# Attention in a hybrid encoder layer: 32 steps with every engine's order written out

## The chip, the cores and the metric

One core of a Trainium2 chip runs the whole layer in one launch. The core has five engines that run side by side, each through its own instruction stream in order: TensorE (PE, matmuls and transposes), VectorE (DVE), ScalarE (ACT), GpSimd (POOL) and SyncE (SP, which here only starts DMAs). The metric is the device time of one execution in microseconds.

## The reference

The layer takes x, 1024 rows by 1024 columns in float32, and does three residual steps and a last norm:

```python
x = x + 0.5 * swiglu_half_step(x, ffn1_norm, ffn1_w_in, ffn1_w_out)
x = x + hybrid_mixer(x, ...)
x = x + 0.5 * swiglu_half_step(x, ffn2_norm, ffn2_w_in, ffn2_w_out)
x = rms_norm(x, final_norm)
```

The mixer projects the normed rows to a query (4 heads of 128), keys and values (2 heads each), and the inputs of a two-way gated recurrence (4 heads of 128). It then computes

```python
attn = rms_norm(softmax(q @ k.T) @ v, attn_out_gain)      # 1024 x 512
rec  = rms_norm(recurrence, rec_out_gain) * silu(g)       # 1024 x 512
return concatenate([attn, rec]) @ w_out                   # 1024 x 1024
```

The feed-forward width is 2816.

## The kernel before, in words

Every matrix product is made of three products of halves: each float32 operand is split into a rounded high part and the rest, and high×high, high×low and low×high are added in the same bank. A split is a cast on ACT and a subtraction on DVE. So twelve matmuls of 128 by 512 make one half of an output projection of 128 rows: 4 heads by 3 products.

The stages follow each other: first FFN, projection and recurrence, attention with both output projections, second FFN. Only the attention stage differs between the two kernels. It works on 32 steps `(tp, n, tt)`: four query tiles of 256 rows, four heads, two halves of 128 rows. One step is

- six score matmuls into `s` (two banks wide, tag "pp"), a row maximum on DVE (`nmax`), the exponential with its sum on ACT (`p`, `den`), the reciprocal on DVE (`rd`), and the scaling of `p`, one half on POOL and the other on ACT;
- eight transposes of `p` in two sets of four (`ptp`, tag "b"), each set split by ACT and DVE into `pT`;
- at the second step of a pair, 24 matmuls `pv` over the values, then gain and split (`oT`) and the squares (`sq`, summed in `ssq`).

Beside the steps lie the other parts of the output. For each of 8 tiles of 128 rows, the recurrence row `rg` (four loads, and one of its gate) is multiplied by the gate on POOL, transposed (`rT`), split (`recT`), projected (`py`, two halves of 12 matmuls) and added to the row `x` from `d["x1"]`; the row goes to `d["x2"]`. For each tile of attention output, `pa` is projected in two halves, scaled by `rs_ao` (from `oss`, the sum of squares) and added to the row from `d["x2"]`. Then `xn` is the normed row for the second FFN. Query tiles are loaded (`qraw`), transposed (`qTp`) and split (`qT`).

The order on each engine is not the order of the code alone: the layer on top of the language reorders the recorded instructions by its own priorities and estimates, so the order that counts is that of the built program. A block under `tc.high_priority()` is pulled forward, and `issue_after` (in the helper `behind`, line 96) keeps an instruction behind another. On-chip memory comes from pools with a number of buffers; a tile that reuses a buffer waits for the last reader of the one before. The output banks are two (tag "o"), the transposes' banks two ("b"), the score banks two ("pp").

In the code below, `softmax` (line 1172) yields between the two halves of the scores; the loop at line 1338 starts the scores two steps ahead (`stage_a(i + 2)`). The recurrence tile i is put out at step i (`rec_out`, line 1265) and both halves of an attention tile at u = 2 or 4 of the next query tile (`attn_out`). Functions that are called but not printed: `split` (cast on ACT, subtraction on DVE), `load_split` (a load and a split), `ps` (a bank of the named tag), and `rstd` (two small operations on DVE and POOL). Line numbers such as L1183 are lines of this kernel.

## Time and profile before

| what | us |
| --- | --- |
| median of 3 runs (1927.78 to 1929.05) | 1928.6 |
| profiled execution, its own time | 1929.75 |
| its span, from first to last instruction | 1927.6 |
| PE busy in the span | 1905.8 |
| attention, from the first scores of step 2 to the end of the last projection | 1054.2 to 1276.2 |

How to read it: busy time is the sum over instructions of an engine; idle time of PE in brackets is put down to what ended it ("<-DVE pT L1206" means that the subtraction of line 1206 was the last thing waited for). In a row of a timeline the first number is the start and the second the length from the first start to the modelled last end, so neighbouring rows on PE overlap a little. "SPq" is SP's queue of DMAs; "landing" counts from issue to the last byte.

### The profile page before, as it was taken

What the parts mean: (1) busy time and instruction counts of PE and PEld (TensorE: products, weight loads), DVE (VectorE), ACT (ScalarE), POOL (GpSimd) and SP (SyncE); (2) the same over time, 40 slices, a digit from 0 to 9 for tenths busy, and PEclk for the clock granted to TensorE, in tenths of its full rate; (3) what the DMA queues carried; (4) which work ended last, traced back from release to release, by engine and by line L of the source; (5) the groups of instructions that cost most, each with busy time, mean ns of one, the idle gap of its engine ahead of it and who ended that gap; (6) DMA issues with size and microseconds to landing.
All of it is one profiled execution on the core that took longest, in us unless ns stands there. A gap on an engine that the chain in (4) does not pass through costs nothing.

```text
span 1927.6 us, 26292 instructions
## 1 busy us (share of the span) xinstructions
PE 1905.8 (99%) x10025; PEld 1597.7 (83%) x10025; DVE 1250.9 (65%) x1578; ACT 802.1 (42%) x1280; POOL 714.1 (37%) x561
## 2 busy tenths in 40 slices
PE   9999999999999999999999999999999999999998
PEld 8888888887888788888888888888888888888886
DVE  8655676655985763677673566657556666558966
ACT  6333343334444432334344455644333333334434
POOL 2664545543670100010001324407554645426701
PEclk9999999999999999999999999999999999999999
DMA  8333333226874411122133452283423332258644
GB/s 263 107 122 106 99 121 101 69 104 245 274 246 133 151 45 44 45 83 83 44 95 111 153 174 77 99 273 99 142 88 109 99 115 82 88 199 297 218 120 164
DMA packets 212940, 254.78 MB, mean 132 GB/s; under 512 B 13495, under 2 KB 140748, under 8 KB 212814
## 3 DMA queue, kind: packets, MB, share of 16 engines
q1 hardware_dynamic: 203758, 222.69, 36.4%
q0 software_dynamic: 9056, 30.42, 4.0%
q8 instruction: 79, 1.29, 0.3%
q14 instruction: 47, 0.39, 0.1%
HBM read 182.79 MB, written 70.25 MB: 131 GB/s over the span
## 4 chain that ended last, share of the span: by engine, by line
PE 90%; DVE 4%; DMA 3%; issue 1%; ACT 1%; POOL 0%; SPq 0%; DVEq 0%; POOLq 0%; ACTq 0%
PE pa_ffn L298 17%; PE pd_ffn L298 11%; PE pya_ffn L684 7%; PE rec_ps L166 6%; PE pc_ffn L298 6%; PE pb_ffn L298 6%; PE pp_ffn L280 5%; PE pye_ffn L684 3%; PE pyd_ffn L684 3%; PE pyc_ffn L684 3%; PE aq_ps L831 2%; PE ri_ps L831 2%; PE pa L1243 2%; PE rgv_ps L831 2%; PE pv L1215 2%; PE s L1183 2%
## 5 line engine op out<-in xcount | busy, mean ns | idle before, releaser
L94 DVE TENSOR_TENSOR hl_in_ffn_A<-raw_in_ffn,hl_in_ffn_A 128x512 fp32r<-128x512 f32 x120 | 177.4, 1478 | 94.0 <-ACT hl_in_ffn_A L93 93.9
L298 PE MATMUL pa_ffn<-ffn_T,hl_in_ffn_S 128*128 128x512 f32 x960 | 236.8, 389 | 0.0
L298 PE MATMUL pd_ffn<-ffn_B,hl_in_ffn_S 128*128 128x512 f32 x936 | 225.7, 389 | 0.0
L298 PEld LDWEIGHTS pa_ffn<-ffn_T,hl_in_ffn_S 128*128 128x128 f32 x960 | 180.2, 188 | 37.4
L298 PEld LDWEIGHTS pd_ffn<-ffn_B,hl_in_ffn_S 128*128 128x128 f32 x936 | 175.7, 188 | 36.4
L93 ACT CAST hl_in_ffn_S<-s_ffn 128x512 fp32r<-128x512 f32 x160 | 99.0, 622 | 212.2 <-PE pd_ffn L298 159.0
L94 DVE TENSOR_TENSOR hl_in_ffn_S<-s_ffn,hl_in_ffn_S 128x512 fp32r<-128x512 f32 x160 | 140.9, 885 | 70.7 <-ACT hl_in_ffn_S L93 70.5
L94 DVE TENSOR_TENSOR hl_out_ffn_A<-raw_out_ffn_A,hl_out_ffn_A 128x1024 fp32r<-128x1024 f32 (+1 forms) x66 | 101.6, 1551 | 48.1 <-ACT hl_out_ffn_A L93 47.3
L93 ACT CAST hl_in_ffn_A<-raw_in_ffn 128x512 fp32r<-128x512 f32 x120 | 74.9, 625 | 137.1 <-PE pc_ffn L298 70.8
L94 DVE TENSOR_TENSOR hl_out_ffn_S<-raw_out_ffn_S,hl_out_ffn_S 128x512 fp32r<-128x512 f32 (+1 forms) x88 | 101.6, 1162 | 40.7 <-ACT hl_out_ffn_S L93 40.7
L166 PE MATMUL rec_ps<-hm,hl_rec_w 128*128 128x512 f32 x528 | 123.1, 392 | 0.8 <-DVE hm L145 0.4
L254 POOL TENSOR_TENSOR s_ffn<-s_ffn,raw_in_ffn 128x512 f32<-128x512 f32 x40 | 63.5, 1587 | 159.5 <-issue 104.6
L684 PE MATMUL pya_ffn<-hl_out_ffn_S 128*128 128x512 f32 x528 | 120.9, 390 | 0.1
L298 PE MATMUL pa_ffn<-ffn_B,hl_in_ffn_A 128*128 128x512 f32 x480 | 116.9, 389 | 0.0
L684 PEld LDWEIGHTS pya_ffn<-hl_out_ffn_S 128*128 128x128 f32 x528 | 99.0, 188 | 21.4 <-DVE hl_out_ffn_S L94 1.0
L166 PEld LDWEIGHTS rec_ps<-hm,hl_rec_w 128*128 128x128 f32 x528 | 98.4, 188 | 21.7 <-DVE hm L145 0.8
L298 PE MATMUL pc_ffn<-ffn_T,hl_in_ffn_A 128*128 128x512 f32 x480 | 115.9, 389 | 0.0
L298 PE MATMUL pb_ffn<-ffn_B,hl_in_ffn_A 128*128 128x512 f32 x480 | 115.3, 389 | 0.0
L93 ACT CAST hl_out_ffn_S<-raw_out_ffn_S 128x512 fp32r<-128x512 f32 (+1 forms) x88 | 73.4, 837 | 95.7 <-PE pya_ffn L684 38.6
L298 PEld LDWEIGHTS pc_ffn<-ffn_T,hl_in_ffn_A 128*128 128x128 f32 x480 | 90.1, 188 | 18.7
L298 PEld LDWEIGHTS pb_ffn<-ffn_B,hl_in_ffn_A 128*128 128x128 f32 x480 | 90.1, 188 | 18.7
L298 PEld LDWEIGHTS pa_ffn<-ffn_B,hl_in_ffn_A 128*128 128x128 f32 x480 | 90.0, 188 | 18.7
(288 smaller groups left out, 3809.4 us busy)
## 6 DMA issues: line engine op xcount, KB each, us to landing
raw_in_ffn<-in_ffn_w_in SPq DMA_DIRECT2D x88, 512.0 KB, 4.2
raw_out_ffn_S<-d_comb SPq DMA_DIRECT2D x88, 256.0 KB, 2.7
d_comb<-g_ffn POOLq DMA_DIRECT2D x80, 256.0 KB, 2.3
raw_out_ffn_A<-d_act SPq DMA_DIRECT2D x66, 256.0 KB, 5.1
ffn_kept<-in_ffn_w_out SPq DMA_DIRECT2D x65, 256.0 KB, 5.4
d_act<-g_ffn SPq DMA_DIRECT2D x60, 256.0 KB, 2.3
raw_out_ffn_A<-in_ffn_w_out SPq DMA_DIRECT2D x52, 256.0 KB, 5.4
x<-d_x SPq DMA_DIRECT2D x24, 512.0 KB, 4.2
```

The lines of the kernel that those rows point to most:

```text
L93: nc.scalar.copy(hl[:, 0, :], src)
L94: (lo_engine or nc.vector).tensor_sub(hl[:, 1, :], src, hl[:, 0, :].bitcast(F32))
L166: nc.tensor.matmul(out, hl[:, a, ks], h[half][b][:, k, cols], start=(k == 0 and i == 0), stop=(k == NK - 1 and i == 2),)
L254: nc.gpsimd.tensor_sub(s2, s1, a11)
L280: nc.tensor.matmul(halves(ps[j]), A[2 * j + k // 4][:, a, ks], B[k // 4][:, :, b, k % 4, lo:hi], start=(k == 0 and i == 0), stop=(k == NK ...
L298: nc.tensor.matmul(ps, A[:, a, ks], op(key)[:, b, k, :], start=(first and k == 0 and i == 0), stop=(k == 3 and i == 2), skip_group_check=True,
L684: nc.tensor.matmul(ps, hl[:, a, j * P : (j + 1) * P], hl[:, b, hi], start=(first and i == 0 and n == 0), stop=(i == last and n == 2), skip ...
L831: nc.tensor.matmul(ps[:, tt, :], h[half][a][:, k, ts], hl[j][:, b, ws], start=(k == 0 and i == 0), stop=(k == NK - 1 and i == 2),)
L1183: nc.tensor.matmul(ps[:, ks], qT[:, a, qs], kT[:, b, kv, ks], start=(i == 0), stop=(i == 2))
L1215: nc.tensor.matmul(ps, vt[:, j, a, vs], pT[j][:, b, i4, :], start=(st == 0 and i == 0), stop=(st == NT - 1 and i == 2),)
L1243: nc.tensor.matmul(py, lhs(a, n), units[n][:, b, ds], start=(n == 0 and i == 0), stop=(n == 3 and i == 2),)
```

## The change

The attention is written as 32 steps in a fixed order. A helper `run` chains each instruction behind the one recorded last on the same engine, so that the order of the code is the order on PE, ACT, DVE and POOL (DMAs are not chained). Within a step: three score matmuls of the step two ahead, four transposes, three more scores; then the small operations; then `oss`, and `pv` of the pair that ended one step earlier; then one of the output parts, either both halves of a recurrence tile (steps 0, 1, 3, 4, 5, 7, 9, 11) or one half of an attention tile (12 steps from 13 on); then the transposes of the next recurrence tile, and half of a query tile's transposes (at u = 2 and 4, in the output banks, where it was all eight in a score bank); then the other four transposes of the step.

The rows of the recurrence part get a second buffer (`x1=2`). The attention weights (`woa`) are requested at steps 2, 5, 8 and 10 and split at 4, 7, 12 and 13. At the end the projections of the last two tiles take heads 0 to 2 first and head 3 after the last `pv`. Instruction counts and sizes stay as they are on PE. In the diff, `free` does the same as `run` without the chain.

```diff
 LEVELS = (1, 2, 4, 8, 16, 32, 64)
+REC_STEPS = (0, 1, 3, 4, 5, 7, 9, 11)
+WOA_LOADS = (2, 5, 8, 10)
+WOA_EARLY = {13: 3}
+WOA_LATE = {4: 0, 7: 1, 12: 2}
+ATTN_HALVES = (13, 15, 16, 17, 19, 21, 23, 25, 27, 28, 29, 31)
...
+        last = {}
+
+        def run(engine, fn, *args, **kw):
+            with self.behind(last.get(engine)):
+                last[engine] = fn(*args, **kw)
+            return last[engine]
+
...
+        def q_turn(do, tp, raw, half, tag):
+            pt = self.ps(f"qTp{tp}_{half}", tag)[:, :512]
+            for m in range(2):
                 for tt in range(2):
-                    o, i = n * 256 + tt * P, tt * 512 + n * P
-                    nc.tensor.transpose(pt[:, o : o + P], raw[:, i : i + P], self.ident)
-            qT = pools["qT"].tile([P, 2, 1024], F32R, name=f"qT{tp}", tag="qT")
-            self.split(qT, pt)
-            return qT
-
-        def softmax(tp, n, tt, qT):
-
-            kv = n // (NQ // NKV)
-            nm = f"{tp}_{n}_{tt}"
...
+        def rec_turn(t):
+            rg = rows[t][0]
+            run("pool", nc.gpsimd.tensor_mul, rg[:, 0:512], rg[:, 0:512], rg[:, 512:])
             pt = self.ps(f"rT{t}", "o")
             for n in range(NREC):
                 ns = slice(n * P, (n + 1) * P)
-                nc.tensor.transpose(pt[:, ns], rg[:, ns], self.ident)
-            rT = pools["rT"].tile([P, 2, 512], F32R, name=f"recT{t}", tag="rT")
-            nc.scalar.mul(rT[:, 0, :], pt, self.rec_gain)
-            nc.vector.scalar_tensor_tensor(
-                out=rT[:, 1, :], in0=pt, scalar=self.rec_gain, in1=rT[:, 0, :].bitcast(F32),
-                op0=ALU.mult, op1=ALU.subtract,
-            )
-            project(
-                lambda a, n: rT[:, a, n * P : (n + 1) * P], units, f"py{t}",
-                lambda ds, py: nc.vector.tensor_add(x1[:, ds], py, x1[:, ds]),
-            )
-            nc.sync.dma_start(d["x2"][t], x1)
-
-        def attn_scale(tp, sq, tag="o"):
+                run("pe", nc.tensor.transpose, pt[:, ns], rg[:, ns], self.ident)
+            rT = recT[t] = pools["rT"].tile([P, 2, 512], F32R, name=f"recT{t}", tag="rT")
+
+            def evacuate():
+                run("act", nc.scalar.mul, rT[:, 0, :], pt, self.rec_gain)
+                run("dve", nc.vector.scalar_tensor_tensor, out=rT[:, 1, :], in0=pt, scalar=self.rec_gain,
+                    in1=rT[:, 0, :].bitcast(F32), op0=ALU.mult, op1=ALU.subtract)
+
+            return evacuate
+
+        def rec_half(t, dd):
+            py = self.ps(f"py{t}_{dd}", "o")
+            half_out(py, lambda x, n: recT[t][:, x, n * P : (n + 1) * P], rec_units, cols(dd))
+            x1 = rows[t][1][:, cols(dd)]
+
+            def evacuate():
+                run("dve", nc.vector.tensor_add, x1, py, x1)
+                if dd:
+                    nc.sync.dma_start(d["x2"][t], rows[t][1])
+
+            return evacuate
+
+        def out_scale(tp, do=run, tag="o"):
...
         for i, (tp, n, tt) in enumerate(seq):
-            if i + 4 < len(seq) and seq[i + 4][1:] == (0, 0):
-                qT[tp + 1] = q_tile(tp + 1)
-            if i + 2 < len(seq):
-                ahead = stage_a(i + 2)
-                next(ahead)
+            a, u = steps[i], i % 8
+            ahead = step(i + 2) if i + 2 < len(seq) else None
             if tt == 0:
-                both = self.hpool.tile([P, 2, 2, 4, 256], F32R, name=f"pT{tp}_{n}", tag="h")
-                pT[i] = [both[:, j] for j in range(2)]
-            pair = i - tt
-            transposed(p[i], pT[pair], tp, n, tt, 0)
-            if i + 2 < len(seq):
-                finish_a(i + 2, ahead)
-            transposed(p[i], pT[pair], tp, n, tt, 1)
-            if tt == 1:
-                values(tp, n, pT[pair], oT[tp], sq[tp])
-            if i < NT:
-                rec_out(i, rec_units, *(loaded if i == 0 else rec_loads(i)))
-            for where in {4: (whl,), 6: (whl,), NT + 1: (whl,), NT + 2: (gate,)}.get(i, ()):
-                self.gate, self.exp = self.step_load, self.last_exp
-                units.append(out_unit(0, len(units), "woa", *where))
-                self.gate = self.exp = None
-            u = i % 8
-            if tp > 0 and u in (2, 4):
-                half = (2, 4).index(u)
-                if half == 0:
-                    scale[tp - 1] = attn_scale(tp - 1, sq[tp - 1])
-                late.append(attn_out(tp - 1, half, oT[tp - 1], scale[tp - 1], units))
-            if tp > 0 and u in (4, 6):
-                half = (4, 6).index(u)
-                to_ffn(2 * tp - 2 + half, late.pop(0))
-
-        def last_scale():
-            if 3 not in scale:
-                with self.tc.high_priority():
-                    scale[3] = attn_scale(3, sq[3], "b")
-            return scale[3]
-
-        attn_out(3, 0, oT[3], last_scale, units, "pp")
-        attn_out(3, 1, oT[3], last_scale, units, "o", self.total)
+                pT = self.hpool.tile([P, 2, 2, 4, 256], F32R, name=f"pT{a.nm}", tag="h")
+            a.pT = pT
+            if u == 0 and tp < 3:
+                raw_q = q_load(tp + 1)
+            if i in WOA_LOADS:
+                j = WOA_LOADS.index(i)
+                raw_w[j] = request(0, j, "woa")
+            if ahead:
+                scores(run, ahead, 0)
+            turned(a, 0)()
+            if i == 0:
+                rec_turn(0)()
+            if i in WOA_EARLY:
+                j = WOA_EARLY[i]
+                units.append(cast(raw_w.pop(j), j, *(gate if j == 3 else whl)))
+            if ahead:
+                scores(run, ahead, 1)
+            if i and i + 1 < len(seq):
+                scaled(run, steps[i + 1])
+            if ahead:
+                exponential(run, ahead)
+            after = []
+            if tp and u == 2:
+                after.append(out_scale(tp - 1))
+            if tt == 0 and waiting:
+                after.append(values(waiting))
+                waiting = None
+            outs = []
+            if i in REC_STEPS:
+                t = REC_STEPS.index(i)
+                if t + 1 < NT:
+                    rows[t + 1] = rec_loads(t + 1)
+                outs = [rec_half(t, dd) for dd in range(2)]
+            elif i in ATTN_HALVES:
+                t, dd = divmod(ATTN_HALVES.index(i), 2)
+                outs = [attn_half(t, dd)]
+            later = []
+            if i + 1 in REC_STEPS:
+                later.append(rec_turn(REC_STEPS.index(i + 1)))
+            if tp < 3 and u in (2, 4):
+                later.append(q_turn(run, tp + 1, raw_q, u // 2 - 1, "o"))
+            tb = turned(a, 1)
+            for f in outs:
+                f()
+            if ahead:
+                inverse(run, ahead)
+            for f in (*after, tb, *later, *finishing):
+                f()
+            finishing = []
+            if i + 1 in ATTN_HALVES[::2]:
+                row(ATTN_HALVES.index(i + 1) // 2)
+            if i - 1 in ATTN_HALVES[1::2]:
+                finishing.append(to_ffn(ATTN_HALVES.index(i - 1) // 2))
+            if i in WOA_LATE:
+                j = WOA_LATE[i]
+                units.append(cast(raw_w.pop(j), j, *(gate if j == 3 else whl)))
+            if tt:
+                waiting = a
+
+        t0 = 2 * (len(seq) // 8 - 1)
+        wide = {}
+        row(t0)
+        for t in (t0, t0 + 1):
+            wide[t] = self.ps(f"pa{t}")
+            for dd in range(2):
+                half_out(wide[t][:, cols(dd)], lhs_attn(t), units, cols(dd), range(3))
+            if t == t0:
+                values(waiting)()
+                finish = to_ffn(ATTN_HALVES.index(len(seq) - 1) // 2)
+        finish()
+        row(t0 + 1)
+        for dd in range(2):
+            half_out(wide[t0][:, cols(dd)], lhs_attn(t0), units, cols(dd), (3,))
+        out_scale(t0 // 2, run, "b")()
+        for dd in range(2):
+            attn_add(t0, dd, wide[t0][:, cols(dd)])
+        nc.gpsimd.dma_start(d["x3"][t0], rows[NT + t0])
+        for dd in range(2):
+            half_out(wide[t0 + 1][:, cols(dd)], lhs_attn(t0 + 1), units, cols(dd), (3,))
+        for dd in range(2):
+            attn_add(t0 + 1, dd, wide[t0 + 1][:, cols(dd)])
+        nc.gpsimd.dma_start(d["x3"][t0 + 1], rows[NT + t0 + 1])
...
-                c3, tc, "m2", rg=2, x1=1, rT=1, p=3, qT=2, qr=1
+                c3, tc, "m2", rg=2, x1=2, rT=1, p=3, qT=2, qr=1```

The built order shows what moved. The first place is PE at the start of the loop, from the scores of step 2 on (`s_1_0` is head 1, half 0; `ptp_0_0_0` the first four transposes of step 0; `py_0` the first half of recurrence tile 0). Before:

```order
L1183 MATMUL s_1_0_8672<-kT,qT_8611 128x512 x6
L1183 MATMUL s_1_1_8741<-kT,qT_8611 128x512 x6
L1202 MATMUL ptp_0_0_0_8677<-ident,p_0_0_8633 128x128 x4
L1202 MATMUL ptp_0_0_1_8696<-ident,p_0_0_8633 128x128 x4
L1183 MATMUL s_2_0_8845<-kT,qT_8611 128x512 x6
L1202 MATMUL ptp_0_1_0_8745<-ident,p_0_1_8649 128x128 x4
L1202 MATMUL ptp_0_1_1_8764<-ident,p_0_1_8649 128x128 x4
L1183 MATMUL s_2_1_8922<-kT,qT_8611 128x512 x6
L1271 MATMUL rT_8704<-ident,rg_8614 128x128 x4
```

Now, the same place:

```order
L1146 MATMUL s_1_0_8677<-kT,qT_8602 128x512 x3
L1146 MATMUL ptp_0_0_0_8681<-ident,p_0_0_8635 128x128 x4
L1146 MATMUL rT_8689<-ident,rg_8617 128x128 x4
L1146 MATMUL s_1_0_8677<-kT,qT_8602 128x512 x3
L1146 MATMUL py_0_8713<-hl_wor_8566,recT_8694 128x512 x3
```

The transposes of the first recurrence tile stand behind three scores and four transposes; before, they stood behind 24 scores and 16 transposes.

The second place is PE in step 4 of the changed kernel, between two sets of transposes (`py_0` and `py_1` are the halves of recurrence tile 3, whose four heads follow each other; `rT_9064` belongs to tile 4, `qTp_1` to the second half of the next query tile):

```order
L1146 MATMUL pv_1_1_9004<-pT_1_0_8828,v_attn 128x256 x24
L1146 MATMUL py_0_9037<-hl_wor_8566,recT_8967 128x512 x3
L1146 MATMUL py_0_9037<-hl_wor_8571,recT_8967 128x512 x3
L1146 MATMUL py_0_9037<-hl_wor_8576,recT_8967 128x512 x3
L1146 MATMUL py_0_9037<-hl_wor_8581,recT_8967 128x512 x3
L1146 MATMUL py_1_9050<-hl_wor_8566,recT_8967 128x512 x3
L1146 MATMUL py_1_9050<-hl_wor_8571,recT_8967 128x512 x3
L1146 MATMUL py_1_9050<-hl_wor_8576,recT_8967 128x512 x3
L1146 MATMUL py_1_9050<-hl_wor_8581,recT_8967 128x512 x3
L1146 MATMUL rT_9064<-ident,rg_9029 128x128 x4
L1146 MATMUL qTp_1_9070<-ident,qraw_8674 128x128 x4
```

All of these use the two output banks, and each waits for the last reader of what stood in its bank before; in the built program `py_1` waits for the add of `py_0`, and `rT_9064` for the add of `py_1`.

The third place is SP's queue at the end of the stage (`x_6` and `x_7` are the last two rows, `xn_` and `raw_in` loads of the second FFN). Before:

```order
L1296 DMA x_5_10602<-d_x_82 128x1024
L1545 DMA xn_3_10888<-d_xn_84 128x1024
L1296 DMA x_6_10768<-d_x_82 128x1024
L1296 DMA x_7_10804<-d_x_82 128x1024
L1545 DMA xn_0_10879<-d_xn_84 128x1024
```

Now:

```order
L1340 DMA x_5_10613<-d_x_82 128x1024
L1664 DMA xn_0_10890<-d_xn_84 128x1024
L1664 DMA xn_1_10891<-d_xn_84 128x1024
L241 DMA raw_in_ffn_0_0_10894<-in_ffn_w_in 128x8x128
L241 DMA raw_in_ffn_0_1_10896<-in_ffn_w_in 128x8x128
L1664 DMA xn_2_10898<-d_xn_84 128x1024
L1664 DMA xn_3_10899<-d_xn_84 128x1024
L241 DMA raw_in_ffn_1_0_10902<-in_ffn_w_in 128x8x128
L241 DMA raw_in_ffn_1_1_10904<-in_ffn_w_in 128x8x128
L1340 DMA x_6_10742<-d_x_82 128x1024
L241 DMA raw_in_ffn_2_0_11453<-in_ffn_w_in 128x8x128
L1340 DMA x_7_10820<-d_x_82 128x1024
```

The two rows moved behind eight and nine loads of the next stage.

More of the change, by code (lines that the diff above doesn't have):

```diff
@@ L1254, in rec_loads, with half_out @@
+            return evacuate
+        def half_out(py, lhs, units, ds, heads=range(4)):
+            for n in heads:
+                for i, (x, y) in enumerate(((0, 0), (0, 1), (1, 0))):
+                    run("pe", nc.tensor.matmul, py, lhs(x, n), units[n][:, y, ds],
+                        start=(n == 0 and i == 0), stop=(n == 3 and i == 2))
+        cols = lambda dd: slice(dd * 512, (dd + 1) * 512)
         def rec_loads(t):
```

257 lines of the change are left out of this document (143 added, 114 removed).

## The prediction

> **What bounds the kernel now.** I read the page first, for the engine that sets the end:
>
> ```profile
> span 1927.6 us, 26292 instructions
> PE 1905.8 (99%) x10025; PEld 1597.7 (83%) x10025; DVE 1250.9 (65%) x1578; ACT 802.1 (42%) x1280; POOL 714.1 (37%) x561
> PE 90%; DVE 4%; DMA 3%; issue 1%; ACT 1%; POOL 0%; SPq 0%; DVEq 0%; POOLq 0%; ACTq 0%
> ```
>
> TensorE is busy for 99% of the span and carries 90% of the chain of waits. The change touches the attention alone, so next come the windows over it (length, then PE, PEld, DVE, ACT and POOL busy, granted clock, DMA share, GB/s):
>
> ```profile
> 1054.20:1151.00 96.80, 94.19 (x539) 80.79 (x538) 58.60 (x87) 51.97 (x88) 32.67 (x24) 1.00 0.51 172
> 1151.00:1235.00 84.00, 81.47 (x513) 71.89 (x512) 55.16 (x86) 51.34 (x96) 34.82 (x34) 1.00 0.24 82
> 1235.00:1276.20 41.20, 39.75 (x232) 33.65 (x231) 22.67 (x40) 18.86 (x36) 10.50 (x12) 1.00 0.54 169
> ```
>
> Of 222.0 us PE is busy 94.19 + 81.47 + 39.75 = 215.4: **6.6 us of idle in the whole attention**. The waits of PE from there to the first matmuls of the second FFN (total, times, longest) name most of it:
>
> ```profile
> PE ptp L1202 <- DVE pT L1206: 3.2, 5, 1.0
> PE s L1183 <- ACT p L1190: 1.0, 2, 0.7
> PE rT L1271 <- issue: 0.9, 1, 0.9
> PE pv L1215 <- DVE pT L1206: 0.7, 2, 0.3
> PE pp_ffn L280 <- DVE ffn_B L388: 0.5, 1, 0.5
> ```
>
> With the last row, 7.1 us can be won. DVE, ACT and POOL have slack, but only if PE meets their results late. The clock is 1.00 throughout.
>
> **What the change costs.** The instructions of PE are the same in number and size, so its work stays and the time moves by the change of its idle: minus 7.1, plus what the new order waits for. Every engine now runs in the recorded order, so a late result stops all that stands behind it.
>
> *Step 0.* PE's row is three scores, four transposes, then the four rT transposes.
>
> ```profile
> 1054.29 2.89 PE L1183 MATMUL s<-kT,qT 128*128 128x512 f32 x12
> 1058.71 1.66 PE L1183 MATMUL s<-kT,qT 128*128 128x512 f32 x6 [0.66 <-ACT p L1190]
> 1062.46 0.60 PE L1271 MATMUL rT<-ident,rg 128*128 128x128 f32 x4
> 1055.11 0.36 SPq L1086 DMA_DIRECT2D d_g<-rg  x1
> 1057.47 0.43 SPq L1260 DMA_DIRECT2D rg<-d_g  x1
> rg<-d_g SPq DMA_DIRECT2D x1, 256.0 KB, 2.8
> 1060.63 1.29 POOL L1267 TENSOR_TENSOR rg<-rg 128x512 f32<-128x512 f32 x1
> ```
>
> Twelve scores take 1057.01 − 1054.29 = 2.72 us (2.89 less the tail that overlaps the next row), 0.227 each. PE is at the rT transposes at 1054.29 + 3 × 0.227 + 0.5 = 1055.5. Their input cannot be there: SP still writes the last gate at 1055.11, issues the gate load at 1057.47, it lands 2.8 later, and the product takes POOL 1.29: 1061.6. PE idles **6.2 us** (6.0 if the load lands sooner, 6.9 if POOL starts at 1060.63 and the 0.9 of issue returns). Before, 12 more scores, 12 more transposes and a wait of 0.66 lay there. Behind rT stand the other scores, the exponential of them and the projection, so nothing can fill it.
>
> *Steps 0 to 13.* The prices of what PE now meets directly (the last row is an add at the end of the stage; its matmuls ended at 1276.18, so a hand-over between engines takes 0.2):
>
> ```profile
> L1273 ACT ACTIVATE recT<-rT,cols 128x512 fp32r<-128x512 f32 x8 | 5.7, 706 | 2.0 <-PE rT L1271 2.0
> L1274 DVE SCALAR_TENSOR_TENSOR recT<-rT,cols,recT 128x512 fp32r<-128x512 f32 x8 | 6.0, 745 | 1.3 <-ACT recT L1273 1.3
> L1280 DVE TENSOR_TENSOR x<-py,x 128x512 f32<-128x512 f32 x16 | 11.0, 690 | 21.8 <-PE py L1243 11.7 <-DMA x<-d_x 5.4 <-PE ptp L1202 4.8
> L1221 ACT ACTIVATE oT<-pv,cols 128x256 fp32r<-128x256 f32 x16 | 7.6, 474 | 25.8 <-PE pv L1215 25.8
> L1230 ACT ACTIVATE sq<-pv 128x256 f32<-128x256 f32 x12 | 4.8, 396 | 1.9 <-DVE oT L1222 1.8
> L93 ACT CAST hl_woa<-raw_woa 128x1024 fp32r<-128x1024 f32 x4 | 4.2, 1053 | 6.4 <-DMA raw_woa<-in_w_out_mix 6.4
> L94 DVE TENSOR_TENSOR hl_woa<-raw_woa,hl_woa 128x1024 fp32r<-128x1024 f32 x4 | 4.9, 1221 | 3.1 <-ACT hl_woa L93 3.1
> 1276.38 0.75 DVE L1299 SCALAR_TENSOR_TENSOR x<-pa,rs_ao,x 128x512 f32<-128x512 f32 x1 [0.62 <-PE pa L1243]
> ```
>
> In step 0 three scores (0.7) cover recT's 0.706 + 0.745: wait 0.75. In step 4 the second py half takes the bank of the first, just ended: its add of 0.69 and two hand-overs of 0.2 stop PE for 1.05 or so, and the next rT waits as long for the second: 2.1. The query transposes of steps 2 and 10 stand in pv's bank, one set of four transposes behind pv: 0.474 + 0.396 + hand-overs − 0.4, 0.95 and 1.15. Step 13's projection needs the weight splits of steps 12 and 13, two casts and two subtractions in a chain with the softmax of the step: 2.2. Smaller ones, recT behind the step's casts on ACT and DVE: 0.6, 0.55, 0.55, 1.8 and 0.55 in steps 3, 5, 7, 9 and 11. The sum is **11.2**. One late engine catches up while PE waits for another, so I take 8.5; the ends are 3 (only steps 4 and 0) and 13.
>
> *Steps 14 to 31.* The bank for the next query transposes in step 18 is that of oss, and rs_ao stands on DVE behind these:
>
> ```profile
> L1205 ACT CAST pT<-ptp 128x512 fp32r<-128x512 f32 x64 | 36.8, 590 | 38.2 <-PE ptp L1202 38.2
> L1206 DVE TENSOR_TENSOR pT<-ptp,pT 128x512 fp32r<-128x512 f32 x64 | 43.2, 685 | 11.6 <-ACT pT L1205 11.2
> L1187 DVE TENSOR_REDUCE nmax<-s 128x1 f32<-128x1024 f32 x30 | 36.5, 1218 | 3.9 <-PE s L1183 3.6
> L1190 ACT ACTIVATE p<-s,nmax 128x1024 f32<-128x1024 f32 x30 | 33.9, 1131 | 0.8 <-DVE nmax L1187 0.8
> L125 DVE SCALAR_TENSOR_TENSOR xn_n<-x,rs_n,g_ffn_norm 128x1024 f32<-128x1024 f32 x6 | 7.7, 1283 | 3.5 <-POOL rs_n L86 3.5
> ```
>
> From the last transposes of step 17: 0.59 + 0.685 + 1.283 (xn) + 0.685 + 1.218 + 1.131 and some 1.0 of read, reciprocal and hand-overs = 6.6; PE has 6 scores, 4 transposes and pv, 4.7: wait 1.9. In the pairs after it, pv's 13th matmul needs the subtraction of the step before, which stands behind a reciprocal, and so behind the exponential; where xn (1.283) lies ahead too, the slack is gone: 0.25 to 1.3 at seven places, 5.5 in all. Sum **7.4**; I take 4.5, ends 1 and 9.
>
> *The tail.*
>
> ```profile
> 1248.41 11.83 SPq L1296 DMA_DIRECT2D x<-d_x  x2
> x<-d_x SPq DMA_DIRECT2D x2, 512.0 KB, 4.1
> 1260.99 1.16 PE L1202 MATMUL ptp<-ident,p 128*128 128x128 f32 x8 [0.18 <-DVE pT L1206]
> 1263.02 3.02 PE L1215 MATMUL pv<-pT,v_attn 128*128 128x256 f32 x23 [0.34 <-DVE pT L1206]
> 1270.59 5.75 PE L1243 MATMUL pa<-hl_woa,oT 128*128 128x512 f32 x24
> 1276.18 1.91 PE L442 MATMUL pt_ffn_B<-ident,xn 128*128 128x128 f32 x16
> 1278.83 1.94 PE L280 MATMUL pp_ffn<-ffn_B,hl_in_ffn_A 128*128 128x256 f32 x14 [0.45 <-DVE ffn_B L388]
> ```
>
> Before, the last two rows of x were requested ahead of the next stage's loads (both by 1259.92, the end of that issue row less 0.3). Now they stand in SP's queue behind xn_0 to xn_3 and four weight loads, x_7 even behind a fifth, which waits for a split on DVE. On DVE the four adds (0.75 each) stand ahead of the ffn_B splits that the first pp needs. Counted from the last ptp (which ends near 1262.0): heads 0 to 2 of pa6 and pv take PE 18 × 0.227 + 2.9 = 7.0; the oT step and two splits behind it (0.5 + 1.4) free SP at about 9; x_7 lands 4.1 later at best, at 13, and at 17 if its load takes twice as long beside four weight loads of its size. The adds cannot start before the sums of oss either, behind x_7's heads 0 to 2 and x_6's last head (24 × 0.227 = 5.4) and 1 of scale: 13.5. Four adds then end at 16.5, or at 18.5 with the late landing; two ffn_B splits and a hand-over bring the first pp to 18 to 20.5, and to 23 if both the splits and xn_5, which stand between on DVE, come late too. PE's own work to there is 24 pv, 48 pa and 16 transposes, 2.9 + 10.9 + 1.9 = 15.7: a wait of 2 to 8. I take **4.5**, nearer the low end, since x_7's landing is the one link that no row prices under this load.
>
> Sum: 6.2 + 8.5 + 4.5 + 4.5 − 7.1 = **+16.6 us**. On the profiled execution's own time of 1929.75 that is 1946.4; the median lies 1.15 below it, so **1945**. With all low ends: 12.2 − 7.1 = +5.1, 1934; with all high ends 36.9 − 7.1 = +29.8, 1958.
>
> **Rivals.**
> *A: not slower.* Scores two steps ahead hide every evacuation, the adds and casts come in time, and only step 0's 6.2 + 0.75 is left against the 7.1 won: 6.95 − 7.1 = −0.15, 1928.4. Faster than that only if the gate load lands sooner too: 1924 with 4 of the 6.2 gone. For it: DVE busy for only 58.60 of 96.80 us. Against: the bank of step 4 is a wait with no work between. Chance 0.17.
> *B: step 0 and the tail alone.* 6.2 + 0.75 + 4.5 − 7.1 = +4.4: 1933. For it: in most steps 2 us of scores and transposes lie between a result and its user. Chance 0.2.
> *C: the forecast*, 0.45.
> *D: the gaps slow PE's restart.* The first transposes of the program and later ones:
>
> ```profile
> 5.83 2.82 PE L1473 MATMUL warm<-ident 128*128 128x128 f32 x12
> 31.96 1.91 PE L442 MATMUL pt_ffn_B<-ident,x_late 128*128 128x128 f32 x16
> ```
>
> At the start one takes 0.235, later 0.12. If each of the two gaps, step 0's and the tail's, cost one to two times what those 12 lost (12 × 0.116 = 1.4), the forecast rises by 3 to 6, to about 1950. No gap inside the attention before is longer than 1.0, so its trace cannot decide. Chance 0.08.
> The Trainium skill (TensorE: Matmul & The Clock Gate, Part 1) says that the clock falls to half after an idle window of about 3.4 us and returns after as long a busy one; the two start rows agree in ratio. By it step 0 alone would cost an estimated 1.7 us more.
> *E: lag adds up.* ACT or DVE falls behind over a pair and no step gives it back: the high ends, 1958. Chance 0.1.
>
> **How the numbers follow.** C is the likeliest, so 1945. Its own range is 1938 to 1952; with B and D inside and the far halves of A and E left out, **1930 to 1957**. About 0.2% (3.9 us) is what can be told from no change. Faster: the part of A in which the early product or the gaps come back, 0.1. Same: the rest of A and a sliver of B, 0.09. Slower: 0.81.
>
> **What would show it.** In the new profile: a gap of about 6 us on PE at the first rT, ended by POOL; PE idle in the attention of 20 us or more against 6.6; py and rT waiting for adds in step 4; the first pp waiting for DVE behind an add of x_7 that a DMA released. I am wrong if the first rT's gap is under 3 us, or if PE's idle there is under 10.

## The result, and the profile after

The changed kernel takes **1954.07 us** (median of 4 runs, 1953.00 to 1954.73) against 1928.52 (4 runs, 1927.78 to 1929.05): a ratio of 1.0132, 95% interval 1.0115 to 1.0150, so 25.5 us slower. The forecast was 1945, 16.5 us slower, with 1930 to 1957 as its range. The direction and the kind of the losses came as forecast; the size did not, and the tail is where most of the difference lies.

The page of the changed kernel, the lines that answer to those of before:

```profile
span 1951.8 us, 26283 instructions
PE 1911.3 (98%) x10025; PEld 1598.6 (82%) x10025; DVE 1251.3 (64%) x1582; ACT 802.0 (41%) x1284; POOL 714.9 (37%) x561
PE 86%; DVE 6%; DMA 3%; ACT 3%; issue 1%; POOL 0%; SPq 0%; DVEq 0%; POOLq 0%; ACTq 0%
```

The span grew by 24.2 us with the same 10025 matmuls; PE's share of the chain fell from 90% to 86%. Where PE waited from the start of the attention to the first matmuls of the second FFN (total, times, longest):

```profile
PE pt_ffn_B L447 <- DVE x L1146: 7.9, 2, 4.5
PE rT L1146 <- POOL rg L1146: 6.0, 1, 6.0
PE qTp L1146 <- DVE rs_ao L1146: 2.0, 1, 2.0
PE qTp L1146 <- ACT ssq L1146: 1.9, 2, 1.1
PE pa L1146 <- DVE hl_woa L1146: 1.2, 2, 0.8
PE py L1146 <- DVE recT L1146: 1.0, 3, 0.3
PE py L1146 <- ACT recT L1146: 1.0, 1, 1.0
PE rT L1146 <- issue: 0.8, 1, 0.8
PE py L1146 <- DVE x L1146: 0.8, 1, 0.8
PE pv L1146 <- DVE pT L1146: 0.6, 2, 0.3
```

Two rows hold 13.9 of some 23 us: the gap of step 0 and the transposes of the second FFN (`pt_ffn_B`), which wait for the adds on the last two rows of x. (L1146 is the line through which every operation of the fixed order is issued; tiles tell them apart.)

**Step 0** on PE, and the granted clock there (windows: length, PE, PEld, DVE, ACT, POOL busy, clock, DMA share, GB/s):

```profile
1061.85 1.12 PE L1146 MATMUL rT<-ident,rg 128*128 128x128 f32 x4 [6.03 <-POOL rg L1146]
1064.05 7.42 PE L1146 MATMUL py<-hl_wor,recT 128*128 128x512 f32 x24
1071.31 0.60 PE L1146 MATMUL rT<-ident,rg 128*128 128x128 f32 x4
```

```profile
1062.00:1066.00 4.00, 4.00 (x12) 3.24 (x13) 1.88 (x2) 2.33 (x3) 1.29 (x1) 0.50 0.35 96
1066.00:1068.00 2.00, 2.00 (x6) 1.56 (x6) 0.00 (x0) 0.86 (x2) 0.00 (x0) 0.56 0.46 125
1068.00:1072.00 4.00, 4.00 (x23) 3.31 (x22) 1.18 (x2) 0.00 (x0) 0.00 (x0) 1.00 0.01 4
```

The gap is 6.03 us long, ended by POOL's product, as forecast. Behind it the clock stands at half for some 5 us, and the 24 matmuls of the first projection take 7.42 us.

**The tail.** SP's queue, then DVE's adds, then PE:

```profile
1259.44 16.61 SPq L1664 DMA_DIRECT2D xn<-d_xn  x2
1276.10 1.28 SPq L241 DMA_DIRECT2D raw_in_ffn<-in_ffn_w_in  x2
1284.68 3.48 SPq L1340 DMA_DIRECT2D x<-d_x  x1
1288.77 1.58 SPq L1340 DMA_DIRECT2D x<-d_x  x1
```

```profile
1293.39 1.41 DVE L1146 SCALAR_TENSOR_TENSOR x<-pa,rs_ao,x 128x512 f32<-128x512 f32 x2 [4.38 <-DMA x<-d_x]
1298.73 1.41 DVE L1146 SCALAR_TENSOR_TENSOR x<-pa,rs_ao,x 128x512 f32<-128x512 f32 x2 [3.93 <-DMA x<-d_x]
```

```profile
1274.99 0.60 PE L1146 MATMUL ptp<-ident,p 128*128 128x128 f32 x4
1300.19 1.12 PE L447 MATMUL pt_ffn_B<-ident,xn 128*128 128x128 f32 x4 [3.37 <-DVE x L1146]
1300.96 3.20 PE L285 MATMUL pp_ffn<-ffn_B,hl_in_ffn_A 128*128 128x256 f32 x15
```

The first pp before:

```profile
1278.00 0.38 PE L280 MATMUL pp_ffn<-ffn_B,hl_in_ffn_A 128*128 128x256 f32 x1
```

And the chain that ended last, over the same stretch:

```profile
1276.57 9.21 DMA raw_in_ffn<-in_ffn_w_in
...
1288.77 9.84 DMA x<-d_x
```

SP stands at the second xn load for 16 us, and what ended most of that is named in the view of SP's waits:

```profile
SPq L1664 <- PE ptp L1146: 15.8, 1, 15.8
```

It waits for the last transposes of p, since the place it loads into still holds the last step's probabilities. Only then do the weights start; they land 9.21 later; the split and xn follow on DVE, then the request of x_7, which lands 9.84 later; and the transposes of the next stage need the banks that x_7's adds still read. From the end of the last score transposes (1274.99 + 0.60) to the first `pp_ffn` it is 25.4 us, for the 15.7 us of PE's own work that the prediction counts there (24 pv, 48 pa, 16 transposes). Before it was 1278.00 − 1262.15 = 15.9, but with 39 of the 48 pa: the other 9 stood ahead of the last score transposes. (The first pp row before is one matmul ahead of the row that the prediction shows.)

### The profile page after: what moved, and what is told of

Read it like the earlier page. It is cut to its first block, busy times and chain, and to the rows that moved or that the text cites. A ratio compares the mean times of both kernels' runs of the same rounds, so it can differ in the third digit from the quotient of the medians.

```text
span 1951.8 us, 26283 instructions
## 1 busy us (share of the span) xinstructions
PE 1911.3 (98%) x10025; PEld 1598.6 (82%) x10025; DVE 1251.3 (64%) x1582; ACT 802.0 (41%) x1284; POOL 714.9 (37%) x561
## 3 DMA queue, kind: packets, MB, share of 16 engines
q8 instruction: 79, 1.29, 0.3%
## 4 chain that ended last, share of the span: by engine, by line
PE 86%; DVE 6%; DMA 3%; ACT 3%; issue 1%; POOL 0%; SPq 0%; DVEq 0%; POOLq 0%; ACTq 0%
PE pa_ffn L303 17%; PE pd_ffn L303 11%; PE pya_ffn L689 7%; PE rec_ps L171 6%; PE pc_ffn L303 6%; PE pb_ffn L303 6%; PE pp_ffn L285 5%; PE pye_ffn L689 3%; PE pyc_ffn L689 3%; PE pyd_ffn L689 3%; PE py L1146 2%; PE aq_ps L836 2%; PE ri_ps L836 2%; PE rgv_ps L836 2%; PE pyb_ffn L689 2%
## 5 line engine op out<-in xcount | busy, mean ns | idle before, releaser
L99 DVE TENSOR_TENSOR hl_out_ffn_S<-raw_out_ffn_S,hl_out_ffn_S 128x512 fp32r<-128x512 f32 (+1 forms) x88 | 108.0, 1239 | 37.8 <-ACT hl_out_ffn_S L98 37.8
L99 DVE TENSOR_TENSOR hl_out_ffn_A<-raw_out_ffn_A,hl_out_ffn_A 128x1024 fp32r<-128x1024 f32 (+1 forms) x66 | 95.7, 1463 | 52.6 <-ACT hl_out_ffn_A L98 51.9
```

What stands on the lines that cost most here:

```text
L99: (lo_engine or nc.vector).tensor_sub(hl[:, 1, :], src, hl[:, 0, :].bitcast(F32))
```

## The experiments

All times are medians; the kernel before, on the same chips, lay at 1928.4 to 1928.8.

**1. The first recurrence tile's loads through POOL's queue.**

```diff
+            q = nc.sync if t else nc.gpsimd
...
-                nc.sync.dma_start(rg[:, n * HD : (n + 1) * HD], d["rec"][n][sl, :])
+                q.dma_start(rg[:, n * HD : (n + 1) * HD], d["rec"][n][sl, :])
...
-            nc.sync.dma_start(rg[:, 512:], d["g"][t // 4][hs, :])
+            q.dma_start(rg[:, 512:], d["g"][t // 4][hs, :])
```

> The changed kernel, but the five loads of the first recurrence row go through POOL's queue instead of SP's, where they stood behind the last gate write; nothing else moves on PE. Theory A (the fixed order puts the first rT transposes ahead of data that a queue brings late, and the idle halves PE's clock afterwards): the gap of 6.0 us in step 0 goes, and with it the 2.9 us that the records show as half clock from 1062 to 1068, so about 9 us: 1945. Rival B (the wait only moves: ACT, DVE and POOL need this time anyway, and later steps wait instead): at most 3 us gained, 1951 or more.

1946.72 (1945.97 to 1947.18), ratio 1.0095 (1.0080 to 1.0110): 7.35 less than the changed kernel, so theory A, 1.7 short of its 9. POOL and PE in this run:

```profile
1047.73 2.24 POOL L1288 DMA_DIRECT2D rg<-d_rec  x4 [4.01 <-DMA d_g<-rg]
1056.99 0.63 PE L1146 MATMUL rT<-ident,rg 128*128 128x128 f32 x4 [0.81 <-issue]
1058.40 6.07 PE L1146 MATMUL py<-hl_wor,recT 128*128 128x512 f32 x24
```

POOL requests the tile at 1047.73; on SP the same five loads stood behind a write that it could only issue at 1055.36. The gap shrinks from 6.03 to 0.81 (5.2 us), and the projection takes 6.07 instead of 7.42. The rest of the 7.35 is clock, which experiment 3 prices.

**2. x_6 and x_7 requested at steps 18 and 20, into the x1 buffers.** The next stage's late rows are also requested behind its second weights.

```diff
-            rows[NT + t] = x = s4(f"x2_{t}", "xs")
+            rows[NT + t] = x = s4(f"x2_{t}", "x1" if t >= 6 else "xs")
...
+            if i in (18, 20):
+                row(6 + (i - 18) // 2)
...
-        row(t0)
...
-        row(t0 + 1)
...
-                load((4, 5, 6, 7))
+                with k.behind(k.last_raw):
+                    load((4, 5, 6, 7))
```

> The changed kernel, but the last two rows x_6 and x_7 are requested in steps 18 and 20 into the free buffers of the x1 rows, and the late loads of the second FFN are held behind its second weights. Theory A (the two rows stand too late in SP's queue and DVE, in order, holds the ffn_B splits behind their adds): the waits of 4.5 and 3.4 us of the first FFN transposes go for the larger part, the first pp comes 4 to 7 us earlier, and the slow clock behind the gap goes too: 1945 to 1950. Rival B (the weights of the second FFN land too late for PE anyway, since all loads share the DMA engines): the wait moves to the weight splits, 1952 or more.

1952.17 (1951.92 to 1953.81): 1.9 less, so theory A's 4 to 7 did not come. The transposes' wait for x fell from 7.9 to 0.8, but new ones stand in its place:

```profile
PE pp_ffn L285 <- DVE ffn_B L393: 2.8, 1, 2.8
PE pp_ffn L285 <- ACT hl_in_ffn_A L393: 2.7, 1, 2.7
```

The early rows took memory into which the next stage's loads go: on SP the fourth xn load waits 18.2 us for the write of x_7, and the second weights behind it are requested at 1296.30 only. That is rival B's time and one of its waits, but not its reason. The run confounds two things: the landing of x_7 is no longer the limit, and something else at once is.

**3. The gap of step 0 filled with 56 transposes of the identity,** whose results are overwritten.

```diff
+            if t == 0:
+                for _ in range(56):
+                    run("pe", nc.tensor.transpose, pt[:, :P], self.ident, self.ident)
```

> The changed kernel with 56 more transposes of the identity into rT's bank ahead of the first rT transposes, which fill most of the 6 us in which PE waits in step 0 and are overwritten. Theory A (PE's clock falls after an idle stretch): the gap stays as long, but what follows it runs at full clock; the 2.9 us at half clock come back: 1951. Rival B (the slow matmuls behind the gap have another cause, such as the loads of that time): no change, 1954.

1953.49 (1952.51 to 1954.54): 0.6 less in all, where theory A said 3. But the row's data came later in this run: the filling ends at 1062.65, the first rT still waits 0.63 for POOL's product, and it starts 1.44 us later than in the changed kernel. What delayed the data was not traced. What the run shows is the work behind:

```profile
1063.29 0.66 PE L1146 MATMUL rT<-ident,rg 128*128 128x128 f32 x4 [0.63 <-POOL rg L1146]
1064.72 6.07 PE L1146 MATMUL py<-hl_wor,recT 128*128 128x512 f32 x24
1070.63 0.60 PE L1146 MATMUL rT<-ident,rg 128*128 128x128 f32 x4
```

From the first rT to the next it takes 1070.63 − 1063.29 = 7.34 us, against 1071.31 − 1061.85 = 9.46 in the changed kernel, with the same work; the clock is 1.00 from 1056 to 1072 here. So **2.1 us are the price of the clock behind the gap**, and 5.2 + 2.1 = 7.3 is what experiment 1 got back.

**4. No fixed order,** the rest of the change kept:

```diff
-            with self.behind(last.get(engine)):
-                last[engine] = fn(*args, **kw)
-            return last[engine]
+            return fn(*args, **kw)
```

> The changed kernel with its code order, its halves, its banks and its places of the output parts, but no chain: the layer on top may reorder every engine as it did before. Theory A (the time is lost by the fixed order in step 0 and the tail): the first rT moves behind more scores and transposes and the step-0 loss of 9 us goes; 1935 to 1946. Rival B (the new grouping itself, banks and halves, costs the time): stays within 3 us of the changed kernel, 1951 or more.

1942.36 (1940.45 to 1943.17), ratio 1.0071 (1.0054 to 1.0088): 11.7 less, inside theory A's range, and still 13.8 more than before. The first rT moves behind 24 scores, as before the change, and no longer waits. PE is busy for 91.44 of the 96.80 us from 1054.20 (86.09 with the order, 94.19 before), and the first pp stands at 1285.65, 7.65 later than before. So the fixed order is less than half of the loss; more remains in what the change does besides.

**5. Early gate load, early rows in other memory, and the next stage's loads in one line.** x_6 and x_7 now go into a buffer of the weights, at step 22; the tiles of p move to the end of the left stack. (The early gate load and the lines that put the loads behind each other are left out here.)

```diff
+            if i == 22:
+                spare = pools["wo"].tile([P, 2, 1024], F32R, name="x67", tag="wo").bitcast(F32)
+                for j in range(2):
+                    rows[NT + t0 + j] = spare[:, j, :]
+                    nc.sync.dma_start(rows[NT + t0 + j], d["x2"][t0 + j])
...
-                c3, tc, "m2", rg=2, x1=2, rT=1, p=3, qT=2, qr=1
+                c3, tc, "m2", rg=2, x1=2, rT=1, qr=1, qT=2, p=3
```

> The early gate load of the first experiment together with the early rows of the second, and, new, the next stage's loads requested one behind the other (the first two normalised rows, the first weights, two more rows, the second weights, the late rows) into memory that the attention has left by then. Nothing of the computation is left out. Theory A (the tail's loss is x_7's late landing plus the bank that its adds hold): both gains add up and the moved wait of the second experiment goes too, so 1954.1 - 7.35 - 1.9 - 2.5 (pp behind hl_in and ffn_B there waited 2.8 and 2.7, of which about half goes) = 1942.3; the waits of the projections' input transposes for x sum to under 1.5 us, against 7.9. Rival B (DVE's order, adds ahead of the splits, sets the first pp whatever lands when): the first pp still waits 4 to 6 us for DVE, and the time is 1954.1 - 7.35 - 1.9 = 1944.8 or more.

1948.82 (1948.19 to 1949.87): theory A missed, and rival B has only its "1944.8 or more", since the first pp waits for ACT and not for DVE. It is 2.1 slower than experiment 1 alone. The waits of PE and of ACT name what stands in the way now:

```profile
PE pp_ffn L287 <- ACT ffn_B L395: 9.1, 1, 9.1
ACT hl_in_ffn_A L395 <- DMA d_x<-x: 13.7, 1, 13.7
```

ACT's casts of the next weights wait for the write of x_6 and x_7 to memory outside, and that write reads nothing but the buffer I gave these rows: so the split weights go into its place. A place taken for one stage is a wait in the next, for the second time. (How much of the 2.1 that is stays open: behind the wait of step 18 the clock also fell in this run's trace and not in experiment 1's, as the last section tells.)

**6. The same, with the tail's banks and order changed.** x_7's halves go to the banks of the score transposes. (The new order of the projections, the sums and the last xn is left out here.)

```diff
-        for t in (t0, t0 + 1):
-            wide[t] = self.ps(f"pa{t}")
+        wide[t0] = self.ps(f"pa{t0}")
...
+        halves = [self.ps(f"pa{t0 + 1}_{dd}", "b") for dd in range(2)]
```

> The kernel of the run before in this list, and besides the tail in another order: the sums for the last scale ahead of x_7's projection, x_7's two halves in banks of the score transposes instead of the wide bank that the next stage's transposes need, and the last normalised row of x_5 behind the adds. Nothing is left out. Theory A (bank held by the adds): the transposes of the second feed-forward no longer wait for x_7's adds; the first pp comes 3 to 4 us sooner than in the run before, about 1939. Rival B (DVE's order): the adds still stand ahead of the splits, so the first pp comes as late as before and only the wait's name changes, from x to ffn_B: within 1 us of the run before.

1945.27 (1943.67 to 1947.69). The transposes wait for x no more, and pp waits 7.9 for ACT ffn_B, where it waited 9.1: the first pp came 1.0 us sooner, against a median 3.6 lower. Of the bank wait only 0.8 was left in experiment 5, and ACT's casts are still held for 11.3 us by the write of the two rows: whether DVE's order would have been the next link, this run cannot tell.

**7. And the query transposes ahead of pv and the projections.** (The lines that put their evacuation ahead of the projections' adds in these steps are left out here.)

```diff
-                after.append(out_scale(tp - 1))
+                after.append(out_scale(tp - 1, run, "b"))
+            if tp < 3 and u in (2, 4):
+                after.append(q_turn(run, tp + 1, raw_q, u // 2 - 1, "o"))
```

> The kernel of the run before in this list, and besides the query transposes of steps 2, 4, 10, 12, 18 and 20 ahead of pv and the projections, with the sums of the scale in a bank of the score transposes, so that these transposes no longer wait for the evacuation of pv or for rs_ao. Nothing is left out. Theory A (each bank wait that is named in the trace costs what its row says): the rows qTp<-ssq 1.9, qTp<-rs_ao 2.0, qTp<-sq 0.2 go, with the waits of step 4 of 0.8 halved: 3.5 to 4.5 us less than the run before. Rival B (PE only catches up on late engines there, so the same lateness appears one row later, at recT, pT or p): under 1.5 us less, and the sum of PE's waits for recT, pT and p grows by 2 us or more.

1944.08 (1942.95 to 1945.21): 1.2 less by the medians, whose ranges overlap; 4.7 less by the two profiled spans. qTp's waits of 4.1 are gone, and oss now waits 2.7 for pT, pa and py 2.1 for qT. That is rival B's picture in the rows; the size stays open, also because the wait in step 18 of experiment 6's trace brought the half clock, some 1.6 us, and is gone here.

**8. Early gate load and the swapped places alone.** Against experiment 1 this is one line:

```diff
-                c3, tc, "m2", rg=2, x1=2, rT=1, p=3, qT=2, qr=1
+                c3, tc, "m2", rg=2, x1=2, rT=1, qr=1, qT=2, p=3
```

> The early gate load of the first experiment, and only the places in memory of the query, transposed-row and probability tiles swapped, so that the second feed-forward's first weights go where the attention ends early; rows x_6 and x_7 are requested as late as in the changed kernel. Nothing is left out. Theory A (the splits of the next stage's first weights stand on DVE behind the adds only where the weights come late): the weights land some 5 us sooner, their splits leave DVE ahead of the adds, but x_7 still lands late, so the transposes still wait for its adds: 1946.7 - 1 to 2.5 = 1944 to 1946. Rival B (the queue of loads is what makes x_7 late, and nothing is gained by the sooner memory): 1946.7 within 1 us.

1937.36 (1936.34 to 1939.15), ratio 1.0045 (1.0030 to 1.0060): **9.4 us less than experiment 1, from where three kinds of tiles lie in memory**. I had expected 1 to 2.5, or nothing. SP and PE in the tail:

```profile
1252.22 0.85 SPq L1665 DMA_DIRECT2D xn<-d_xn  x2
1253.16 2.86 SPq L241 DMA_DIRECT2D raw_in_ffn<-in_ffn_w_in  x2
1268.21 0.34 SPq L1341 DMA_DIRECT2D x<-d_x  x1
1280.10 0.34 SPq L1341 DMA_DIRECT2D x<-d_x  x1
```

```profile
1267.78 0.60 PE L1146 MATMUL ptp<-ident,p 128*128 128x128 f32 x4
1285.84 0.66 PE L447 MATMUL pt_ffn_B<-ident,xn 128*128 128x128 f32 x4 [1.05 <-DVE x L1146]
1286.25 0.36 PE L285 MATMUL pp_ffn<-ffn_B,hl_in_ffn_A 128*128 128x256 f32 x1
```

In experiment 1 the same stretch on PE reads:

```profile
1268.30 0.60 PE L1146 MATMUL ptp<-ident,p 128*128 128x128 f32 x4
1294.32 3.50 PE L285 MATMUL pp_ffn<-ffn_B,hl_in_ffn_A 128*128 128x256 f32 x15
```

The second xn load no longer stands for 16 us; the first weights are requested 16 us sooner than in experiment 1 (1253.16, there 1269.41), x_6 is requested before the last transposes are through, and x_7 11.7 us behind them, and its adds ran at 1284.37. From the last score transposes to the first pp it is 1286.25 − 1268.38 = 17.9 us, with experiment 1's 1294.32 − 1268.90 = 25.4: 7.5 of the 8.9 by which the two traced spans differ (1935.3 and 1944.2). Some 0.5 lie ahead of this stretch and 0.8 behind it; the clock stays at 1.00 from 1268 to 1290. The order of the requests did not get better: x_6 stands behind eight of the next stage's loads as in experiment 1, x_7 behind ten instead of nine. So it is the places.

**9. One buffer for the x1 rows again,** the rest of the change kept:

```diff
-                c3, tc, "m2", rg=2, x1=2, rT=1, p=3, qT=2, qr=1
+                c3, tc, "m2", rg=2, x1=1, rT=1, p=3, qT=2, qr=1
```

> The changed kernel with one part undone: one buffer for the rows x1 instead of two. This shortens the left stack of the attention by one place of 4 KB a partition, so the probabilities' tiles lie one place lower, where they lay before the change. Nothing is left out. Theory M (the tail's loss is mostly that the second buffer pushes the probabilities onto the place where the second feed-forward's second normalised row and first weights are loaded, which then wait for the last step's probabilities): the tail gets back what the swap of places got back with the early gate load, 9.4 us, less what late x1 rows now cost in steps 1 and 4 (0 to 4 us): 1945 to 1949, with the gap of 6.0 at the first rT still there, and the next stage's rows and weights requested before the last transposes of p. Rival N (it was the swap's order of SP's queue, not the place): 1954 or more, since the x1 loads can only come later.

1950.30 (1947.52 to 1951.16): 3.8 less than the changed kernel, 1.3 outside theory M's range and 3.7 from rival N's. SP's waits:

```profile
SPq L1664 <- PE ptp L1146: 6.8, 1, 6.8
SPq L241 <- PE ptp L1146: 3.2, 1, 3.2
```

15.8 became 6.8 and 3.2, and the transposes' wait for x 4.5 instead of 7.9. With one buffer the probabilities' tiles still lie under part of the next loads. So the second buffer made the conflict worse; it did not make all of it. (In this run's trace the clock also fell behind the wait of step 18, which cost 1.6 there and nothing in the changed kernel.)

**10. Query transposes first in their step, the sums one step earlier, splits half a step earlier,** on top of experiment 8.

```diff
-WOA_EARLY = {13: 3}
-WOA_LATE = {4: 0, 7: 1, 12: 2}
+WOA_EARLY = {12: 2}
+WOA_LATE = {4: 0, 7: 1, 12: 3}
...
+            if tp < 3 and u in (2, 4):
+                q_turn(run, tp + 1, raw_q, u // 2 - 1, "o")()
...
-            if tp and u == 2:
+            if tp and u == 1:
...
-            if tp < 3 and u in (2, 4):
-                later.append(q_turn(run, tp + 1, raw_q, u // 2 - 1, "o"))
```

> The kernel with the early gate load and the swapped places, and besides: the query transposes of steps 2, 4, 10, 12, 18 and 20 first in their step, the sums for the scale one step earlier, and the last two weight splits of the output projection half a step earlier. Nothing is left out. Theory A (each wait costs what its row says): the rows qTp<-rs_ao 2.0, qTp<-ssq 2.0, pa<-hl_woa 1.2 and qTp<-sq 0.2 go: 1937.4 - 5.4 = 1932. Rival B (the engines behind are late there, so another instruction waits instead): 1936 or more, and new waits of the same sum for pT, recT, qT or x.

1941.24 (1938.92 to 1943.27): 3.9 more than experiment 8, so rival B, and dearer than it said. The rows that were aimed at are gone; the sums now wait for POOL, 5.0 us at three places, the longest here:

```profile
1236.82 1.01 PE L1146 MATMUL oss<-ones,ssq 128*128 128x1 f32 x4 [2.96 <-POOL ssq L1146]
1237.69 5.45 PE L1146 MATMUL pa<-hl_woa,oT 128*128 128x512 f32 x12
1238.80:1240.80 2.00, 2.00 (x6) 1.54 (x5) 0.00 (x0) 0.91 (x2) 0.00 (x0) 0.50 0.00 0
```

In experiment 8 the same half projection took 2.89 for its 12 matmuls. So a gap of 2.96 cost 2.96 + 2.56. Behind the sums' wait of 1.06 at 1132.56 the clock fell too (0.60 from 1134 to 1138), and half a projection took 4.58.

**11. The kernel before, with two x1 buffers and nothing else.**

```diff
-                c3, tc, "m2", rg=2, x1=1, rT=1, p=3, qT=2, qr=1
+                c3, tc, "m2", rg=2, x1=2, rT=1, p=3, qT=2, qr=1
```

> The kernel before the change with one part of the change alone: two buffers for the rows x1 instead of one; the order stays the scheduler's. Nothing is left out. Theory M (the second buffer pushes the probabilities onto the place of the next stage's first loads): the loads of the second feed-forward's rows and weights wait for the last transposes of p at about 1262, their splits come 2 to 6 us late, and the first pp with them: 1931 to 1935. Rival N (the place of p matters only behind a fixed order, because the scheduler's own order and the early requests of x_6 and x_7 leave slack): 1928.5 within 1.5.

1933.52 (1932.31 to 1934.69, 7 runs), ratio 1.0025 (1.0014 to 1.0037): **a second buffer alone makes the old kernel 5.1 us slower**. The time is theory M's, its mechanism is not: the first pp stands at 1277.38, no later than before (1278.00). The loss shows 20 us behind it:

```profile
1297.54 1.06 ACT L388 ACTIVATE ffn_T<-x_late 128x1024 fp32r<-128x1024 f32 x1 [3.99 <-DMA x_late<-d_x]
PE pp_ffn L280 <- DVE t_ffn L220: 1.3, 1, 1.3
1310.00:1314.00 4.00, 4.00 (x11) 3.09 (x12) 4.00 (x6) 4.00 (x9) 4.00 (x4) 0.62 0.34 100
```

ACT waits 3.99 for the last row of the next stage, 0.50 before the change; DVE's next splits follow, PE waits 0.6, 0.6 and 1.3 where it waited for nothing before, and the clock falls to 0.62. By the traced spans (1931.0 and 1927.6) the loss is 3.4, all of it behind the first pp; the rest of the 5.1 is in the medians only. Which place in memory delays that load was not traced, and so stays open.

**12. No fixed order, with the swapped places** (experiments 4 and 8 together, without the early gate load).

```diff
-            with self.behind(last.get(engine)):
-                last[engine] = fn(*args, **kw)
-            return last[engine]
+            return fn(*args, **kw)
...
-                c3, tc, "m2", rg=2, x1=2, rT=1, p=3, qT=2, qr=1
+                c3, tc, "m2", rg=2, x1=2, rT=1, qr=1, qT=2, p=3
```

> The changed kernel without the fixed order on the engines (as in the fourth experiment), with the swapped places of memory besides. Nothing is left out. Theory M (memory's part of the tail is the same whatever the order): 1942.4 - 8 = 1934, with the first pp within 2 us of where it stands before. Rival N (without the fixed order the scheduler already works round the late loads): 1942 within 2.

1934.73 (1933.64 to 1936.94), ratio 1.0035 (1.0021 to 1.0048): 7.6 less than experiment 4, theory M's time. Its second condition failed: the first pp stands at 1283.64, 2.0 sooner than in experiment 4 but still 5.6 later than before; most of the gain lies behind it. This is the fastest of the changed versions, and none beats the kernel before.

## Why the prediction was right or wrong

In the middle column is what was taken; on the right what the rows or the runs show.

| step of the sum | taken | measured |
|---|---|---|
| step 0, gap at the first rT | 6.2 | 6.0 gap, and 2.1 of half clock behind it |
| steps 0 to 13 | 8.5 (sum of the rows 11.2) | 6.9 (1.9 + 1.2 + 1.0 + 1.0 + 0.8 + 0.8 + 0.2) |
| steps 14 to 31 | 4.5 (sum 7.4) | 2.8 (2.0 + 0.6 + 0.2) |
| tail | 4.5, ends 2 and 8 | 25.4 − 15.7 = 9.7 (waits of 4.5 and 3.4, and 1.8 more, much of it at half clock) |
| idle of before | −7.1 | −7.1 |
| sum | +16.6 | +20.4, of 24.2 measured in the spans |

Of the 3.8 that carry no row, 2.6 lie ahead of the first pp (22.96 later than before, 20.4 named) and 1.2 behind it, where the clock is still 0.68.

**Step 0 was right.** SP's queue held the loads behind the last gate write, PE waited 6.03, and POOL's product ended it. Experiment 1 took the cause away and the gap went. What the text left to a rival was the clock: D said 3 to 6 us for two gaps, with a chance of 0.08. It was no rival at all, since it needs nothing but C's own gaps; it belonged in the sum. Experiment 3 prices the first at 2.1, in D's range of one to two times 1.4. Of the Trainium skill's rule (TensorE: Matmul & The Clock Gate, Part 1), cited there with an estimated 1.7, the trace agrees in kind: half clock behind the 6.03 gap, and full again within some 5 us.

**The two middle terms were too high, not wrong.** The wait for rs_ao in step 18 was forecast at 1.9 and is 2.0; those behind pv in steps 2 and 10 at 0.95 and 1.15, and are 1.1 and 0.8; step 4 at 2.1, and is 0.8 + 0.8 + 0.2. The weight splits of step 13 were forecast at 2.2 and took 1.2. What failed is the list of small ones: of seven places at which pv was to wait for pT, two did, for 0.6 together. What I added up there was hidden by the scores two steps ahead, as rival A said.

**The tail is the step that failed**, by 5.2 us of 9.7: its waits of 7.9 lie just inside the high end of 8, and the slower work behind them was in no term. Next comes the 2.1 of clock behind step 0's gap; the middle terms, 3.3 too high, hid part of both. The tail's links were right: x_7 behind a load that waits for a split on DVE, adds ahead of the next stage's work. The sizes were not. "The oT step and two splits behind it free SP at about 9" measured 13.2 us from the last ptp (1288.77 − 1275.59), and x_7's landing, put at 4.1 to 8 us, took 9.84. Behind both lies a wait that the text never looked for: SP stood 15.8 us before the second xn load, because the place it loads into is that of the last probabilities, so all loads of the next stage fell into the time in which x_7 was to land. I followed the order of the queue row by row and never asked where each of its loads goes. Experiment 8 moved only the places and got 9.4 back. It was also said that ffn_B's splits behind the adds set the first pp; in the row it is the transposes themselves that wait, for the banks of x_7's projection. DVE's first splits do start right behind the adds, at 1300.06, so without the bank the first pp could hardly have come much sooner; no run tells the two apart.

**The rest.** Against 25.5 stand 7.35 for step 0 (experiment 1), 9.4 for the places (8 against 1), and 8.8 that experiment 8 still loses. Of those its PE rows name most: they sum to 12.8 up to the first pp, against 7.1. Without the fixed order, and with the same places, it is 2.6 less (12 against 8), so the order itself costs little once its two long waits are gone. What the last 6.2 of experiment 12 are was not settled; the second x1 buffer, which cost the kernel before 5.1, is still in it. Attempts to remove the small waits one by one (7, 10) moved them to the next row.

**Rivals.** A failed at step 0's clock, in the middle steps and at the tail. B left out the middle steps, which cost 9.7. E's time (1958) came near, by another way: the rows show single waits, not a lag that grows over a pair.

## What to carry to other kernels

For each load that crosses from one stage to the next, ask what lies in its place and when that is last read, not only where it stands in its queue: adding a buffer to one pool moves all behind it, and one queue in order turns a late place into lateness for everything behind it. Price a gap on TensorE at its length, and reckon with more for the clock behind it: 2.1 and 2.56 us behind the gaps of 6.03 and 2.96 here, and behind one of 1.97 either nothing or some 1.6. When removing a wait that is one of several on engines that are late together, expect the next row to wait instead.
